# A hybrid decoder step on one core: when VectorE gets the next MLP weights' remainders, when the decode is held, and half of the split keys read back from memory

## The chip, the cores and the metric

The kernel runs on one core of a Trainium2 chip. The core has a matrix engine (TensorE; "PE" in the profile, its weight loads "PEld"), VectorE (DVE), ScalarE (ACT), GpSimd (POOL) and SyncE (SP), which here only issues transfers. Transfers are issued by SyncE, ScalarE and GpSimd into queues of their own, and 16 DMA engines carry them out. The metric is the device time of one execution in microseconds. The kernel before was run three times.

## The reference, cut to what matters

One layer of a decoder with width 1024 is computed for two groups of rows which share the weights: a prompt of 1024 tokens, and 8 samples of one token each with a cache of 8192 past tokens in pages of 128.

```python
h = rmsnorm(x) @ w_in                      # q, k, v (8 heads x 64), a forget logit per head, u, z
att = softmax(q k^T / 8 + c_q - c_k) v     # c: running sum of log_sigmoid(forget logit); causal
sgu = gelu(u) * (W_s z + b_s)              # gating in chunks of 128
x  += concat(rmsnorm(att), rmsnorm(sgu)) @ w_o
x  += cross_attention(rmsnorm(x)) @ w_co   # 4 heads into 256 memory tokens
h   = causal_conv3(rmsnorm(x) @ w_up)      # 2 x 2816 columns
x  += (silu(gate) * val) @ w_down
y   = rmsnorm(x)
```

All of it is float32. The keys, values, log forget gates, memory keys and values and the last convolution rows are returned too.

## The kernel before, in words

**Splitting.** A float32 product is made of three products of a faster format (`gemm3`, lines 265 to 272): each operand is split into a head `h`, a rounded copy made by ScalarE (line 233, or 236 with a scale), and a remainder `l = src - h`, made by VectorE (line 234 or 237). `wload` (line 250) loads a weight tile through SyncE into one of four `wr` buffers (line 247) and splits it into `wh` (five buffers) and `wl` (four).

**The prompt** goes through stages, in two halves of 512 tokens where this is possible: the input projections with the statistics of the norm (`p1`), attention of half 0 (`att0`, mixed with the memory's keys and values and the gating), attention of half 1 (`att1`), and then for each half `mid0`/`mid1` (merging of the heads, `out_proj` with `w_o`, cross-attention, `out_proj` with `w_co`) and `ffn0`/`ffn1` (the MLP, `ffn`). Half 1's merge is made beside the last `w_down` tiles of half 0's MLP (`side`).

**A stage's end.** `out_proj` makes the output in two column halves `n` of four row tiles `i`. Each tile's sum is added to the residual on VectorE (`residual`, line 953) and squared on ScalarE (line 228). Then `norm_T` (line 1016) transposes the result for the next product: TensorE's transposes (line 1028, and 1044 for the last row tile), each then split by ScalarE (line 236) and VectorE (line 237), first 8 times for the 384 columns of three row tiles, then 8 times for the last 128. The caller gives `first`, the next stage's first product, which is made on those columns as soon as they are there. In `ffn` this is tile 0 of `w_up`; the next tiles in its loop are 22, 1 and 23, as the gate's tiles (0 to 21) and the value's (22 to 43) alternate.

**Attention.** For each pair of heads `load` fetches queries, keys and values and `setup` prepares them: it transposes the queries (line 701) and the keys (line 726), splits them (ScalarE 707, 708, 730, GpSimd 732 or ScalarE 734; VectorE 721, 737), and fills in rows with the forget gates' sums by GpSimd's queue (709, 718). `setup` is a generator; the loop over the pair before advances it by a step after each score tile. Half 1 needs all 1024 keys, and there `setup` does the same to keys 0 to 511 (`kh == 0`) as half 0 did, and then to 512 to 1023. Raw keys, values, prepared operands and probabilities lie in 18 buffers `u` of 1024 columns; queries, small probabilities (the score tiles of half 0 among them) and outputs in 7 buffers `t2` of 520 columns. Half 1's first pair is prepared during half 0's last.

**The decode** of the 8 samples is a generator of its own (`sample`): 128 key steps and 128 value steps, each of which gathers 1 MB of the cache by an indirect transfer on GpSimd's queue (1333 and 1392) into one of four `kv` buffers. A key step multiplies on VectorE (line 1339) and reduces (line 1343); a value step is four matmuls (line 1398). Then come the samples' own projections (`sample_rest`).

**What sets the order.** The prompt is a generator too, and each of its yields tells how many microseconds of work it stands for. The loop at the end of `build` adds these up in `acc` and, whenever they reach the stage's `PACE`, takes a step from the decode, with at most `int(t / PACE) + 1` steps at one yield. While `held[0]` is set it takes none: from the last tile of an `out_proj`, and from the second half's first tile at the end of half 0's MLP, until `norm_T` ends or the stage is over. What was not taken stays in `acc`. The order in which instructions are traced is only their priority: a planner runs a cost model over the program, gives out buffers, and writes down one fixed order for each engine, in which an instruction that is ready sooner by that model may go ahead of one traced earlier. `tc.issue_after(x)` puts the instructions of a block behind `x` in their engine's order, without waiting for `x` to finish; the decode's key steps are put behind VectorE's newest instruction in this way (`behind`).

Of the kernel before, what the change touches and what calls it, by code (L numbers as in the profile page):

```python
# [79 lines left out]
def build(nc, tc, ctx, a, phases=None):  # L80
# [127 lines left out]
    cq_d = dram.tile([NH, 4, T], F32, tag="cq_d", name="cq_d")  # L208
    ck_d = dram.tile([NH, 4, T], F32, tag="ck_d", name="ck_d")
    an_d = dram.tile([T, AW], F32, tag="an_d", name="an_d")  # L210
    qs_d = dram.tile([NB, AW], F32, tag="qs_d", name="qs_d")
# [17 lines left out]

    def split(src, h, l, scale=None):  # L230

        if scale is None:
            nc.scalar.activation(h, src, AF.Copy)  # L233
            nc.vector.tensor_tensor(l, src, h.bitcast(F32), op=ALU.subtract)  # L234
        else:
            nc.scalar.activation(h, src, AF.Copy, scale=scale)
            nc.vector.scalar_tensor_tensor(l, src, scale, h.bitcast(F32), op0=ALU.mult, op1=ALU.subtract)  # L237
# [11 lines left out]

    def wload(src, n, raw=None):  # L250

        if raw is None:
            raw = wraw(src, n)
        l = spool.tile([P, SWID], F32R, tag="wl", bufs=WL, name=nm("wl"))[:, :n]
        h = spool.tile([P, SWID], F32R, tag="wh", bufs=WH, name=nm("wh"))[:, :n]
        if len(src.shape) == 3:
            h = h.rearrange("p (a b) -> p a b", b=src.shape[2])
            l = l.rearrange("p (a b) -> p a b", b=src.shape[2])
        split(raw, h, l)
        return h, l, raw  # L260
# [420 lines left out]
    def attention(hf, late=None, at=3):  # L681
# [3 lines left out]
        def load(hp):  # L685
            cs = slice(hp * P, (hp + 1) * P)
            qn = T2().rearrange("p (i c) -> p i c", c=P)
            nc.sync.dma_start(qn, q_d[hf * 512 : (hf + 1) * 512, cs].rearrange("(i p) c -> p i c", p=P))
            if hf == 0:
                kvn = U([P, 2 * nk, P])  # L690
                kn, vn = kvn[:, :nk, :], kvn[:, nk:, :]
            else:
                kn, vn = U([P, nk, P]), U([P, nk, P])
            nc.sync.dma_start(kn, k_d[: nk * P, cs].rearrange("(i p) c -> p i c", p=P))
            nc.sync.dma_start(vn, v_d[: nk * P, cs].rearrange("(i p) c -> p i c", p=P))
            return qn, kn, vn

        def setup(hp, qn, kn, vn):
# [4 lines left out]
            for j in range(2):  # L703
# [7 lines left out]
                if hf == 0:  # L711
                    kab = U([P, 2, 512], F32R)
                    ka.append(kab[:, 0, :])
                    kb.append(kab[:, 1, :])
                else:
                    ka.append(U([P, nk * P], F32R))
                    kb.append(U([P, nk * P], F32R))
                nc.gpsimd.dma_start(kb[j][64:68, :], ck_d[h, :, : nk * P])
            for j, qq in enumerate(qab):
                rows = slice(64 * j, 64 * j + 64)  # L720
                nc.vector.tensor_tensor(qq[64:128, 0, :], tr[rows, :], qq[0:64, 0, :].bitcast(F32), op=ALU.subtract)
            for kh in range(hf + 1):
                yield
                tr = (MS, BB, BA)[SB]()
                for i in range(4):
                    nc.tensor.transpose(tr[:, i * P : (i + 1) * P], kn[:, kh * 4 + i, :], ident)
                s = slice(kh * 512, kh * 512 + 512)
# [7 lines left out]
                for j in range(2):  # L735
                    rows = slice(64 * j, 64 * j + 64)
                    nc.vector.tensor_tensor(kb[j][0:64, s], tr[rows, :], ka[j][0:64, s].bitcast(F32), op=ALU.subtract)
            got.append((qab, ka, kb, vn))

# [221 lines left out]
    def out_proj(w, mh, ml, xt, fetch=None, ys=None):  # L961
# [19 lines left out]
        for n in range(2):  # L981
# [16 lines left out]
            for i in range(4):  # L998
# [14 lines left out]

                held[0] = n == 1 and i == 3
                yield 5.2 if n else 0.1
# [164 lines left out]
    def ffn(hf, xt, ys, late=None):  # L1180
# [5 lines left out]

        hs, ls = yield from norm_T(ys, G_FFN, lambda hs, ls, c: up(pv0[:, c], w0, hs, ls, c))
        if hf:
# [10 lines left out]
        for gi, gn in enumerate(GROUPS):  # L1199
            gh, gl = [], []  # L1200
            for f in range(f0, f0 + gn):
                hc2 = []
                for part in range(2):
# [3 lines left out]
                    if ft:  # L1207
                        w_, pv = wload(a["w_up"][ft], 1024), BK()
                        up(pv, w_, hs, ls, slice(0, 512))
                    else:  # L1210
                        pv = pv0
# [20 lines left out]
            for n in range(2):  # L1232
# [9 lines left out]
                for i in range(4):  # L1242
# [3 lines left out]
                    if f0 + gn < NF:  # L1246
                        xs_ = xt[i][:, n * 512 : (n + 1) * 512]
                        nc.vector.tensor_tensor(xs_, ps[:, :512], xs_, op=ALU.add)
                    else:
                        residual(xt, sq, i, n, ps)  # L1250
                    yield 3.9
                    if side and n:

                        held[0] = True
                        for _ in range(2):
# [546 lines left out]
    bgs.append(sample())  # L1802
    seen = 0
    for t in prompt():
# [6 lines left out]
        acc[0] += t  # L1811
        most = int(t / PACE[phase[1] or phase[0]]) + 1
        while bgs and not held[0] and most and acc[0] >= PACE[phase[1] or phase[0]]:
            most -= 1
            acc[0] -= PACE[phase[1] or phase[0]]
            w = next(bgs[0], None)
            if w is None:
                bgs.pop()
            else:
                acc[0] -= (w - 1) * PACE[phase[1] or phase[0]]  # L1820
        seen = len(nc.cur_bb.bb.instructions)
# [92 lines left out]
```

## Time and profile before

| | |
|---|---|
| time, median of 3 runs | 1885.33 us (1883.57 to 1890.65) |
| the profiled execution's own time | 1887.23 us |
| its span, first to last instruction | 1885.5 us |
| TensorE busy | 1810.9 us (96%) |
| VectorE busy | 1400.3 us (74%) |
| ScalarE busy | 755.7 us (40%) |
| GpSimd busy | 478.6 us (25%) |
| mean granted TensorE clock | 0.980 |
| moved by DMA | 517 MB, 274 GB/s |

All times within the execution are microseconds from the span's start. A timeline's line gives start, length, engine, line of the kernel, operation, output and inputs, and in brackets the engine's idle time before it with what ended it. A line of the waits gives who waited for whom, with total, times and longest. A line of the stretches gives the length, the busy time of each engine with its instructions, the granted clock of TensorE as a share of full speed, the DMA engines' share and the rate. Matmuls overlap, so that one of 512 columns is shown with 0.39 us or more although the next starts 0.23 us after it.

Where the stages lie in the trace: attention of half 0 up to about 390, of half 1 to 520, `w_o` of half 0 to 573, its cross-attention from there, `w_co` to 739, the MLP of half 0 to 1173, `w_o` of half 1 to 1228, `w_co` to 1393, the MLP of half 1 to the end.

### The profile page before, as it was taken

What the parts mean: (1) busy time and instruction counts of PE and PEld (TensorE: products, weight loads), DVE (VectorE), ACT (ScalarE), POOL (GpSimd) and SP (SyncE); (2) the same over time, 40 slices, a digit from 0 to 9 for tenths busy, and PEclk for the clock granted to TensorE, in tenths of its full rate; (3) what the DMA queues carried; (4) which work ended last, traced back from release to release, by engine and by line L of the source; (5) the groups of instructions that cost most, each with busy time, mean ns of one, the idle gap of its engine ahead of it and who ended that gap; (6) DMA issues with size and microseconds to landing.
All of it is one profiled execution on the core that took longest, in us unless ns stands there. A gap on an engine that the chain in (4) does not pass through costs nothing.

```text
span 1885.5 us, 24204 instructions
## 1 busy us (share of the span) xinstructions
PE 1810.9 (96%) x9255; PEld 1298.5 (69%) x9255; DVE 1400.3 (74%) x1672; ACT 755.7 (40%) x1371; POOL 478.6 (25%) x429
## 2 busy tenths in 40 slices
PE   8999999888898999999999999999999999999998
PEld 5987676556676667776777776765675668667765
DVE  4888678776687887889989898898865549654344
ACT  5332356565633444433324235234443333232232
POOL 1232332232121423313422322243322021101110
PEclk9999999988998999999999999999999999999999
DMA  8877888753396877659878888889869587678871
GB/s 319 286 259 269 326 314 290 287 182 105 132 384 229 328 272 280 257 201 375 301 280 314 284 320 328 344 319 349 308 242 346 196 294 260 253 218 286 321 253 59
DMA packets 156372, 517.07 MB, mean 274 GB/s; under 512 B 20168, under 2 KB 41928, under 8 KB 123488
## 3 DMA queue, kind: packets, MB, share of 16 engines
q0 software_dynamic: 56400, 339.04, 48.4%
q1 hardware_dynamic: 92944, 163.89, 25.1%
q10 hardware_dynamic: 6912, 12.59, 1.8%
q8 instruction: 73, 1.20, 0.2%
q14 instruction: 43, 0.35, 0.1%
HBM read 493.63 MB, written 21.84 MB: 273 GB/s over the span
## 4 chain that ended last, share of the span: by engine, by line
PE 84%; DVE 6%; DMA 4%; ACT 3%; issue 2%; POOL 1%; SPq 0%; DVEq 0%; POOLq 0%; ACTq 0%
PE ba L270 13%; PE ba L271 13%; PE ba L272 12%; PE bb L270 7%; PE bb L271 7%; PE bb L272 7%; PE dv L1398 6%; DVE kv L1339 1%; PE dv L1648 1%; DVE s L1343 1%; PE bb L796 1%; PE ba L994 1%; PE ba L996 1%; PE ba L995 1%; DMA wr<-w_ck 1%
## 5 line engine op out<-in xcount | busy, mean ns | idle before, releaser
L233 ACT ACTIVATE wh<-wr 128x1024 fp32r<-128x1024 f32 (+2 forms) x220 | 228.6, 1043 | 514.8 <-PE ba L271 173.5
L234 DVE TENSOR_TENSOR wl<-wr,wh 128x1024 fp32r<-128x1024 f32 (+2 forms) x220 | 263.1, 1201 | 127.5 <-PE ba L272 55.0
L1339 DVE TENSOR_TENSOR kv<-kv,d 128x1024 f32<-128x1024 f32 (+1 forms) x184 | 295.5, 1634 | 27.3 <-DMA kv<-cache_k,kidx 27.1
L1333 POOL DMA_INDIRECT kv<-cache_k,kidx x128 | 175.0, 1367 | 552.8 <-DVE s L1343 257.6
L1343 DVE TENSOR_REDUCE s<-kv 128x16 f32<-128x1024 f32 (+1 forms) x184 | 296.6, 1626 | 0.2
L1392 POOL DMA_INDIRECT kv<-cache_v,kidx x128 | 179.0, 1399 | 388.2 <-DVE s L1343 178.7
L270 PE MATMUL ba<-wh,u 128*128 128x512 f32 (+1 forms) x601 | 229.7, 384 | 3.1 <-DVE u L953 2.7
L271 PE MATMUL ba<-wl,u 128*128 128x512 f32 (+1 forms) x601 | 227.7, 379 | 0.0
L272 PE MATMUL ba<-wh,u 128*128 128x512 f32 (+1 forms) x601 | 224.9, 379 | 0.0
L270 PE MATMUL ba<-u,wh 128*128 128x512 f32 (+2 forms) x520 | 204.4, 394 | 0.4 <-DVE u L237 0.4
L271 PE MATMUL ba<-u,wh 128*128 128x512 f32 (+2 forms) x520 | 204.5, 394 | 0.0
L272 PE MATMUL ba<-u,wl 128*128 128x512 f32 (+2 forms) x520 | 203.2, 391 | 0.0
L1398 PE MATMUL dv<-kv,s 128*32 128x512 f32 x1024 | 136.5, 614 | 5.5 <-DMA kv<-cache_v,kidx 5.5
L270 PE MATMUL bb<-u,wh 128*128 128x512 f32 (+2 forms) x344 | 138.6, 403 | 0.7 <-DVE u L237 0.7
L270 PEld LDWEIGHTS ba<-wh,u 128*128 128x128 f32 x601 | 113.3, 189 | 37.6 <-issue 10.7
L271 PE MATMUL bb<-u,wh 128*128 128x512 f32 (+2 forms) x344 | 136.8, 399 | 1.5 <-DVE u L237 1.5
L272 PE MATMUL bb<-u,wl 128*128 128x512 f32 (+2 forms) x344 | 135.8, 395 | 0.0
L272 PEld LDWEIGHTS ba<-wh,u 128*128 128x128 f32 x601 | 113.1, 188 | 26.5 <-issue 5.0
L271 PEld LDWEIGHTS ba<-wl,u 128*128 128x128 f32 x601 | 113.3, 189 | 23.1 <-issue 2.5
L271 PEld LDWEIGHTS ba<-u,wh 128*128 128x128 f32 x520 | 99.3, 191 | 32.0 <-issue 12.2
L270 PEld LDWEIGHTS ba<-u,wh 128*128 128x128 f32 x520 | 99.3, 191 | 31.4 <-issue 8.4
L272 PEld LDWEIGHTS ba<-u,wl 128*128 128x128 f32 x520 | 99.1, 191 | 27.8 <-issue 8.0
(422 smaller groups left out, 3066.1 us busy)
## 6 DMA issues: line engine op xcount, KB each, us to landing
wr<-w_up SPq DMA_DIRECT2D x88, 512.0 KB
kv<-w_up POOLq DMA_DIRECT2D x22, 1024.0 KB, 6.7
wr<-w_down SPq DMA_DIRECT2D x40, 512.0 KB
kv<-w_down POOLq DMA_DIRECT2D x11, 1024.0 KB, 7.8
wr<-w_in SPq DMA_DIRECT2D x16, 512.0 KB
wr<-w_o SPq DMA_DIRECT2D x16, 512.0 KB
wr<-w_cq SPq DMA_DIRECT2D x16, 512.0 KB
wr<-w_co SPq DMA_DIRECT2D x16, 512.0 KB
```

What stands on the lines that cost most here:

```text
L233: nc.scalar.activation(h, src, AF.Copy)
L234: nc.vector.tensor_tensor(l, src, h.bitcast(F32), op=ALU.subtract)
L270: mmul(out, sh, mh, start=(i == 0), stop=False)
L271: mmul(out, sh, ml, start=False, stop=False)
L272: mmul(out, sl, mh, start=False, stop=(i == n - 1))
L796: mmul(po[64 * j : 64 * j + 64, q0:256], vn[:, kt, 64 * j : 64 * j + 64], pt[j][kt // 4][:, kt % 4, q0:256], start=(kt == 0), stop=(kt == ...
L994: mmul(pss[i], mh[k][:, tb], wh, start=(k == korder[0]), stop=False)
L1333: nc.gpsimd.indirect_dma_start(kv, None, a["cache_k"], off(kidx[:, b, ch : ch + 1]))
L1339: nc.vector.tensor_tensor(kvv[:, i : i + m, :], kvv[:, i : i + m, :], qb.unsqueeze(1).broadcast_to((P, m, 512)), op=ALU.mult)
L1343: nc.vector.tensor_reduce(s[:, ch * 4 + i : ch * 4 + i + m, :].rearrange("p k h -> p (k h)"), kvv[:, i : i + m, :].rearrange("p k (h d) -> ...
L1392: nc.gpsimd.indirect_dma_start(kv, None, a["cache_v"], off(kidx[:, b, ch : ch + 1]))
L1398: mmul(dv[32 * j : 32 * j + 32, :], s[:, ch * 4 : ch * 4 + 4, :].rearrange("p k h -> p (k h)"), kvv[:, j, :], start=(ch == 0), stop=(ch == ...
```

## The change

There are four parts.

1. `ffn` issues the loads of `w_up` tiles 22, 1 and 23 ahead of `norm_T`, and puts VectorE's subtraction for them behind marks: that of tile 22 behind VectorE's newest instruction after `first` on the first 384 columns, those of 1 and 23 behind its newest after `first` on the last 128. ScalarE's rounded copies are not bound.
2. The hold begins a tile sooner: in `out_proj` at `n == 1, i == 2`, and at the end of half 0's MLP with the last tile of `n == 0`.
3. The loop that takes decode steps has a `credit`: it grows with the prompt's yields, up to 1.2 paces (or one yield), and each step costs 0.75 of a pace; a step is taken only if it is there.
4. Half 0's attention stores the split keys of its 512 tokens (head and remainder) in a DRAM tile `ks_d`, by four transfers on GpSimd's queue for each pair. Half 1 reads them back on SyncE's queue, three transfers of 64 rows of 2 KB for each head (the head part twice), and transposes and splits only keys 512 to 1023. Its raw keys are half as many and lie in a `t2` buffer, not in a `u` buffer.

```diff
-    def split(src, h, l, scale=None):
+    def split(src, h, l, scale=None, after=None):
         if scale is None:
             nc.scalar.activation(h, src, AF.Copy)
-            nc.vector.tensor_tensor(l, src, h.bitcast(F32), op=ALU.subtract)
+            with tc.issue_after(after) if after else nullcontext():
+                nc.vector.tensor_tensor(l, src, h.bitcast(F32), op=ALU.subtract)
...
-                kn, vn = U([P, nk, P]), U([P, nk, P])
-            nc.sync.dma_start(kn, k_d[: nk * P, cs].rearrange("(i p) c -> p i c", p=P))
+                kn, vn = T2().rearrange("p (i c) -> p i c", c=P), U([P, nk, P])
+            nc.sync.dma_start(kn, k_d[hf * 512 : nk * P, cs].rearrange("(i p) c -> p i c", p=P))
...
                     ka.append(U([P, nk * P], F32R))
                     kb.append(U([P, nk * P], F32R))
+                    for r in range(2):
+                        nc.sync.dma_start(ka[j][64 * r : 64 * r + 64, 0:512].bitcast(F32), ks_d[h, :, 0, :])
+                    nc.sync.dma_start(kb[j][0:64, 0:512].bitcast(F32), ks_d[h, :, 1, :])
...
-            for kh in range(hf + 1):
+            for kh in (hf,):
...
+            if hf == 0:
+                for j in range(2):
+                    nc.gpsimd.dma_start(ks_d[hp * 2 + j, :, 0, :], ka[j][0:64, :].bitcast(F32))
+                    nc.gpsimd.dma_start(ks_d[hp * 2 + j, :, 1, :], kb[j][0:64, :].bitcast(F32))
...
-                held[0] = n == 1 and i == 3
+                held[0] = n == 1 and i >= 2
...
-        hs, ls = yield from norm_T(ys, G_FFN, lambda hs, ls, c: up(pv0[:, c], w0, hs, ls, c))
+        order = [f + part * NF for f in range(2) for part in range(2)][1:]
+        raws = {ft: wraw(a["w_up"][ft], 1024) for ft in order}
+        marks = []
+
+        def first(hs, ls, c):
+            up(pv0[:, c], w0, hs, ls, c)
+            marks.append(newest(ENG.DVE))
+
+        hs, ls = yield from norm_T(ys, G_FFN, first)
+        after = dict(zip(order, (marks[0], marks[1], marks[1])))
...
-                        w_, pv = wload(a["w_up"][ft], 1024), BK()
+                        w_, pv = wload(a["w_up"][ft], 1024, raws.pop(ft, None), after.pop(ft, None)), BK()
...
+                    held[0] = side is not None and (n == 1 or i == 3)
                     yield 3.9
                     if side and n:
-                        held[0] = True
...
-    seen = 0
+    seen, credit = 0, 0.0
...
-        most = int(t / PACE[phase[1] or phase[0]]) + 1
-        while bgs and not held[0] and most and acc[0] >= PACE[phase[1] or phase[0]]:
+        pace = PACE[phase[1] or phase[0]]
+        most, credit = int(t / pace) + 1, min(credit + t, max(1.2 * pace, t))
+        while bgs and not held[0] and most and acc[0] >= pace and credit >= 0.75 * pace:
             most -= 1
-            acc[0] -= PACE[phase[1] or phase[0]]
+            acc[0] -= pace
+            credit -= 0.75 * pace
```

More of the change, by code (lines that the diff above doesn't have):

```diff
@@ L209, in build @@
     ck_d = dram.tile([NH, 4, T], F32, tag="ck_d", name="ck_d")
+    ks_d = dram.tile([NH, 64, 2, 512], F32, tag="ks_d", name="ks_d")
     an_d = dram.tile([T, AW], F32, tag="an_d", name="an_d")
@@ L248, in wraw, with wload @@
         return raw
-    def wload(src, n, raw=None):
+    def wload(src, n, raw=None, after=None):
         if raw is None:
@@ L258, in wload @@
             l = l.rearrange("p (a b) -> p a b", b=src.shape[2])
-        split(raw, h, l)
+        split(raw, h, l, after=after)
         return h, l, raw
@@ L725, in setup @@
                 for i in range(4):
-                    nc.tensor.transpose(tr[:, i * P : (i + 1) * P], kn[:, kh * 4 + i, :], ident)
+                    nc.tensor.transpose(tr[:, i * P : (i + 1) * P], kn[:, i, :], ident)
                 s = slice(kh * 512, kh * 512 + 512)
@@ L1819, in build @@
             else:
-                acc[0] -= (w - 1) * PACE[phase[1] or phase[0]]
+                acc[0] -= (w - 1) * pace
         seen = len(nc.cur_bb.bb.instructions)
```

## The prediction

> **What bounds the kernel now.** I read the page first (busy shares, the clock row, the chain that ended last), then the busy time by stretch, then what TensorE waited for at each stage's end, and last the timelines of VectorE and TensorE there.
>
> ```profile
> span 1885.5 us, 24204 instructions
> PE 1810.9 (96%) x9255; PEld 1298.5 (69%) x9255; DVE 1400.3 (74%) x1672; ACT 755.7 (40%) x1371; POOL 478.6 (25%) x429
> ...
> PEclk9999999988998999999999999999999999999999
> ...
> PE 84%; DVE 6%; DMA 4%; ACT 3%; issue 2%; POOL 1%; SPq 0%; DVEq 0%; POOLq 0%; ACTq 0%
> ```
>
> TensorE is busy for 96% of the span and is 84% of the chain, so the change can win only where TensorE stands still or runs at a lower granted clock: 1885.5 - 1810.9 = 74.6 us of idle time. The next rows say where (columns: length, busy us of PE, PEld, DVE, ACT, POOL, clock, DMA share, GB/s).
>
> ```profile
> 400.00:520.00 120.00, 102.09 (x660) 72.21 (x661) 78.77 (x111) 70.38 (x143) 27.25 (x32) 0.89 0.43 147
> 573.00:603.00 30.00, 23.23 (x119) 19.53 (x117) 25.48 (x41) 9.93 (x22) 2.98 (x3) 0.83 0.58 198
> 739.00:759.00 20.00, 16.43 (x93) 14.36 (x91) 14.09 (x27) 11.71 (x27) 3.29 (x3) 0.91 0.59 211
> 1158.00:1180.00 22.00, 19.30 (x107) 13.79 (x107) 22.00 (x25) 14.14 (x26) 9.13 (x6) 1.00 0.91 330
> 1222.00:1250.00 28.00, 25.73 (x144) 18.61 (x142) 26.33 (x37) 12.03 (x23) 10.76 (x9) 0.94 0.85 305
> 1392.00:1412.00 20.00, 18.83 (x112) 15.79 (x111) 10.26 (x22) 11.63 (x24) 1.67 (x2) 1.00 0.50 202
> ...
> 759.00:1158.00 399.00, 398.95 (x1857) 289.26 (x1855) 365.12 (x339) 136.49 (x209) 113.80 (x82) 1.00 0.81 297
> ```
>
> The first row is the second half's attention; the next five are the five stage ends that the change touches: 30 - 23.2 = 6.8 us idle, then 3.6, 2.7, 2.3 and 1.2. Lower clock costs more: 30 x (1 - 0.83) = 5.1 us, 1.8, 0, 1.7, 0. The attention stretch has 17.9 idle and 120 x 0.11 = 13.2 of clock. In the last row, the first half's MLP, TensorE is never idle.
>
> **The change part by part.** *The remainders (MLP start).* Before, three `w_up` tiles beyond the first (22, 1, 23) have their remainder (line 234) taken on VectorE as soon as they land, in the middle of the stage end:
>
> ```profile
> 733.64 2.35 DVE L1339 TENSOR_TENSOR kv<-kv,d 128x1024 f32<-128x1024 f32 x2
> 739.17 1.22 DVE L234 TENSOR_TENSOR wl<-wr,wh 128x1024 fp32r<-128x1024 f32 x1
> 740.30 1.22 DVE L1343 TENSOR_REDUCE s<-kv 128x16 f32<-128x1024 f32 x1
> 741.43 1.22 DVE L234 TENSOR_TENSOR wl<-wr,wh 128x1024 fp32r<-128x1024 f32 x1
> 742.56 0.69 DVE L953 TENSOR_TENSOR u<-bb,u 128x512 f32<-128x512 f32 x1
> 743.16 1.22 DVE L234 TENSOR_TENSOR wl<-wr,wh 128x1024 fp32r<-128x1024 f32 x1
> ...
> 738.58 0.40 PE L271 MATMUL bb<-wl,u 128*128 128x512 f32 x1
> 738.81 0.40 PE L272 MATMUL bb<-wh,u 128*128 128x512 f32 x1
> 743.30 0.55 PE L1028 MATMUL bb<-cp,u 128*128 128x128 f32 x3 [2.45 <-DVE u L953]
> ...
> 738.15 6.58 SPq L247 DMA_DIRECT2D wr<-w_up  x4
> ```
>
> TensorE ended the last tile at 739.2, but its residual (line 953) started at 742.56: two remainders and half a decode reduction stood before it, and a third remainder behind it, ahead of the splits of the next transposes. TensorE waits 2.45 us for that residual's bank. After the change neither the three remainders nor this decode step (held, below) is there; line 953 can start near 739.2, 3.3 us sooner. The whole loss is 3.6 + 1.8 = 5.4; ScalarE, busy 11.7 of these 20 us, is late next, so I take 4.0 (0 to 5.4). At the other MLP start no key step is left and the idle is 1.2, so 0.8 (0 to 1.2). The early loads cost nothing: SyncE's four `w_up` loads were already issued at 738.15, before the transposes.
>
> The price: tiles 1 and 23 now have no remainder until the last of the 16 `norm_T` splits.
>
> ```profile
> 751.41 0.35 DVE L237 SCALAR_TENSOR_TENSOR u<-ba,gp,u 128x128 fp32r<-128x128 f32 x1 [0.99 <-ACT u L236]
> ...
> 758.70 0.35 DVE L237 SCALAR_TENSOR_TENSOR u<-ba,gp,u 128x128 fp32r<-128x128 f32 x1 [0.91 <-ACT u L236]
> ```
>
> Until then TensorE has tile 22 (24 matmuls, 0.23 us from start to start as at 738.58 and 738.81, 5.6 us) and the first tile's last 128 columns with their transposes (some 4 us), against the chain of these eight splits, 751.4 to 759.1. That cover nearly suffices; without it TensorE would wait for two remainders at 1.22 us, 2.4 per start. I take 0.5 at each, 1.0 in all (0 to 4.8).
>
> *The hold.* I counted decode steps through the loop's rule: when the hold begins at the five ends, 46, 62, 104, 112 and 129 steps have been issued before, 45, 61, 103, 110 and 128 after. So one key step leaves each of the first three ends (two line 1339 of 1.17 us and as much again in line 1343, some 4.5 us of VectorE) and two the fourth; at the fifth all 128 key steps are past. The first:
>
> ```profile
> 575.15 2.35 DVE L1339 TENSOR_TENSOR kv<-kv,d 128x1024 f32<-128x1024 f32 x2
> 577.42 1.13 DVE L237 SCALAR_TENSOR_TENSOR u<-ba,gp,u 128x384 fp32r<-128x384 f32 x2
> ...
> 578.08 1.54 PE L1028 MATMUL ba<-cp,u 128*128 128x128 f32 x6 [2.25 <-DVE u L237]
> 580.33 0.69 PE L270 MATMUL bb<-u,wh 128*128 128x384 f32 x1 [0.71 <-DVE u L237]
> 590.02 0.33 PE L1044 MATMUL bb<-cp,u 128*128 128x128 f32 x1 [2.19 <-DVE u L237]
> ```
>
> With that step gone the first two waits (2.25 + 0.71) should go, and their share of the clock loss, 5.1 x 2.96/6.8 = 2.2: 5.2 at most. The third stays, as the held step is the one that follows there next. I take 4.0 (0 to 5.2). At the end of the first MLP:
>
> ```profile
> 1162.20 2.33 DVE L1339 TENSOR_TENSOR kv<-kv,d 128x2048 f32<-128x2048 f32 x1
> 1170.29 2.25 DVE L1343 TENSOR_REDUCE s<-kv 128x32 f32<-128x2048 f32 x1
> 1173.20 0.50 PE L270 MATMUL ba<-wh,u 128*128 128x512 f32 x1 [2.53 <-DVE u L953]
> ```
>
> Two key steps overlap here; the hold, two tiles sooner, takes the second out: 2.5 (0 to 2.7). At the fourth end (1222 to 1250) VectorE is still working through steps issued well before the hold, as their loads came late (DMA share 0.85), so I take 1.0 of its 2.3 + 1.7 (0 to 4.0).
>
> *The even follow.* It spends the backlog at 1/0.75 of the pace at most. By my count the decode's main part ends 4 yields of the prompt later (index 403 for 399), the last step one sooner (460 for 461, of 470). What is moved goes to stretches where TensorE was never idle: 0. VectorE has 399 - 365 = 34 us free in the first MLP for one more step of 4.5 us.
>
> *The split keys.* The second half no longer transposes and splits the first 512 keys. In a head pair's preparation that work stands alone in the chain that ended last (start, length):
>
> ```profile
> 408.21 0.60 PE ba L726 x4
> 408.84 0.60 ACT u L730
> ...
> 410.79 0.69 DVE u L737
> ...
> 442.90 0.59 PE ba L726 x4
> ...
> 476.33 0.60 PE ba L726 x4
> ```
>
> Four transposes 0.6, two copies 1.2, two subtractions 1.4: 3.3 us from 408.21 to 411.48, in each of three pairs (the others begin at 442.90 and 476.33); the first pair, prepared during the first half, has the two copies to lose, 1.2: 11 at most. The least is the transposes alone, 4 x 0.6 = 2.4. GpSimd's eight copies go too. I take 6, about the middle, since the pair before can fill a part with its scores. New work: in the first half 16 stores on GpSimd's queue, at the price of the nearest issue there (below, 0.55 each, 9 us, GpSimd busy 25%), each behind VectorE's subtraction; only decode loads queue behind, and the decode gets 6 steps in that stage. In the second, 24 loads of 128 KB on SyncE, 3 MB less the 1 MB of keys no longer read, at a DMA share of 0.43: 0.
>
> ```profile
> L709 POOL DMA_DIRECT2D u<-cq_d x16: 518/555/642, 144.4 to 469.9; - x16
> ...
> 346.20 13.34 SPq L688 DMA_DIRECT2D t<-q_d  x2
> 392.25 0.38 SPq L688 DMA_DIRECT2D t<-q_d  x1
> ...
> 367.31 0.90 PE L780 MATMUL bb<-cp,t 128*128 128x128 f32 x3 [3.06 <-ACT t L759]
> ```
>
> The keys' raw tile moves to the `t2` pool of seven, which is short: a query load into it held SyncE's queue 13 us at 346, the next went out only at 392. Behind it wait the values and the next pair's loads. I take 1.0; the bound is the slower rival's.
>
> **The sum.** 4.0 + 0.8 + 4.0 + 2.5 + 1.0 + 6.0 = 18.3 gained, 1.0 + 1.0 lost: 16.3. The profiled execution took 1887.23, 1.9 above the median 1885.33; 1887.2 - 16.3 = 1870.9, and 1869 for the median.
>
> **A rule against part of this.** The row 573 to 603 has its clock at 0.83 though no single wait in it exceeds 2.25 us, and I counted clock as won back. The Trainium skill, TensorE: Matmul & The Clock Gate, Part 1: The HAM clock gate, says that the clock halves only after an idle window of about 3.4 us. By that rule closing short gaps gives back idle alone, the second rival below; the trace's row speaks rather against it.
>
> **The rivals.** (1) The preparation of keys is off the path: only 2.4 of the 6 comes, 1872.6. For it: VectorE, busy 78.8 of those 120 us, can put a decode step into the same place; against it: the chain rows above. (2) Gaps this short cost only themselves: without clock 2.5 and 3.0 at the two large ends, 4 in attention: 2.5 + 3.0 + 0.8 + 2.5 + 1.0 + 4.0 - 2.0 = 11.8, 1873.5. (3) ScalarE becomes the late one at the ends: about 1.0, 0.4, 1.0, 1.0, 0 there and 2.4 in attention, less 2.0: 3.8, 1881.5, no measurable change. For it: each transpose passes through its copy before VectorE's split; against it: it is busy 9.9 of 30 us at the first end. (4) Slower: the keys' raw tile holds a `t2` slot from about 360, the end of that 13 us wait, to its transposes, while the first half's last pair needs one for each of its eight score tiles. If each then opens a gap like the 3.06 us at 367, with clock in the stretch's proportion (13.2/17.9), that is 8 x 3.06 x 1.74 = 42 us, against the gain 1885.3 - 17.3 + 42 = 1910. Three gaps (16 us) eat the gain; it is slower by 0.5% from five on.
>
> **How the numbers follow.** 0.5% (9.4 us) is about what a measurement of this kernel can tell from no change. Forecast 0.40, rival 1 0.15, rival 2 0.10, rival 3 0.22, rival 4 0.13. Faster is the first three, 0.65; same 0.22; slower 0.13. All upper ends together are 29.5 gained, 1856; 4 more of the attention's clock, 1852, is the low end. The high end, 1892, holds rival 3 and the first gaps of rival 4. The forecast's own range is 1856 to 1876.
>
> **What would show it.** Right: at the MLP starts line 953 follows the last matmul within a microsecond, two line-234 subtractions come behind the last split; no line 1339 between the first projection's end and line 237; the attention stretch several microseconds shorter, with half of line 730's copies gone there. Wrong: TensorE waiting for line 234 behind the splits, for ScalarE at the ends, or for scores in 355 to 400 with SyncE held on `t2`.

## The result: slower, and the profile after

The changed kernel takes 1901.69 us (median of 5 runs, 1897.28 to 1903.98), the kernel before beside it 1886.02 (5 runs, 1883.57 to 1890.65): ratio 1.0069, 95% interval 1.0050 to 1.0089. That is 13 us slower by the ratio, where 16 us less were forecast, and beyond the range given. Below, a ratio times 1886 is written as microseconds.

The page of the changed kernel, whose profiled execution took 1903.98 us:

```profile
span 1902.2 us, 24264 instructions
...
PE 1816.6 (95%) x9239; PEld 1296.1 (68%) x9239; DVE 1393.8 (73%) x1664; ACT 751.7 (40%) x1365; POOL 477.5 (25%) x437
...
PE 77%; DMA 7%; DVE 7%; issue 5%; ACT 3%; POOL 1%; SPq 0%; DVEq 0%; POOLq 0%; ACTq 0%
```

TensorE's idle time is 1902.2 - 1816.6 = 85.6 us (74.6 before), and it is busy 5.7 us longer although it has 16 instructions less. So the loss has two parts, and only the larger one is idle time. The stretches of the changed kernel at the same places as those shown of before (the same columns):

```profile
400.00:520.00 120.00, 105.79 (x704) 76.08 (x705) 80.39 (x115) 74.12 (x149) 24.05 (x29) 0.93 0.61 194
561.00:591.00 30.00, 22.57 (x109) 18.03 (x108) 27.22 (x40) 11.58 (x23) 3.73 (x3) 0.83 0.60 202
739.00:759.00 20.00, 15.86 (x87) 13.85 (x85) 12.08 (x24) 10.89 (x26) 1.56 (x2) 0.91 0.23 80
1156.00:1178.00 22.00, 20.89 (x113) 15.55 (x112) 21.27 (x25) 14.19 (x26) 5.87 (x5) 1.00 1.02 388
1222.00:1250.00 28.00, 24.47 (x140) 18.20 (x139) 27.56 (x39) 10.70 (x22) 8.18 (x7) 1.00 0.81 298
1600.00:1620.00 20.00, 14.40 (x44) 9.59 (x43) 20.00 (x27) 4.20 (x7) 2.17 (x3) 0.79 0.60 189
```

Attention (first row) gained what the kept keys promised: 14.2 us idle for 17.9, the clock 0.93 for 0.89. The first two stage ends (second and third row) did not gain at all: 7.4 us idle for 6.8 and 4.1 for 3.6, at the same clocks. The end of the first MLP gained 1.6, the fourth end lost 1.3 of idle time and won back 1.7 of clock. And the last row is new: in the second MLP, where the kernel before has this,

```profile
1600.00:1620.00 20.00, 19.60 (x86) 15.55 (x85) 20.00 (x26) 7.94 (x11) 2.15 (x3) 1.00 0.51 170
```

TensorE now stands still for 5.6 us and its clock is at 0.79. The timeline of TensorE in the changed kernel shows for whom it waits:

```profile
1604.84 0.50 PE L272 MATMUL ba<-wh,u 128*128 128x512 f32 x1 [0.78 <-ACT u L234]
...
1606.73 0.49 PE L273 MATMUL ba<-wl,u 128*128 128x512 f32 x1 [1.39 <-DVE wl L236]
...
1607.39 0.50 PE L272 MATMUL ba<-wh,u 128*128 128x512 f32 x1 [0.17 <-DVE t L1235]
...
1615.10 1.22 PE L274 MATMUL ba<-wh,u 128*128 128x512 f32 x2 [2.00 <-DVE u L236]
...
1618.01 0.79 PE L272 MATMUL ba<-wh,u 128*128 128x512 f32 x1 [1.27 <-DVE t L1235]
```

And that of VectorE shows what stood in its way there, lines 1587 and 1589, the product and the sums of the sample's cross-attention with its memory keys:

```profile
1607.33 2.33 DVE L1589 TENSOR_REDUCE sS<-kv 128x4 f32<-128x1024 f32 x2
...
1610.31 2.35 DVE L1587 TENSOR_TENSOR kv<-kv,d 128x1024 f32<-128x1024 f32 x2
...
1613.24 1.21 DVE L236 TENSOR_TENSOR wl<-wr,wh 128x1024 fp32r<-128x1024 f32 x1
...
1614.97 2.33 DVE L1589 TENSOR_REDUCE sS<-kv 128x4 f32<-128x1024 f32 x2
```

VectorE is full (20.00 of 20). The remainder for which TensorE waits at 1615.10 is made at 1614.37, directly behind the one at 1613.24, and has had two such pairs in front of it. The generator of the sample gives each of these eight steps the weight 3 (it yields 3). The loop charges the backlog `acc` three paces for it, but the new `credit` only 0.75 of one.

### The profile page after: what moved, and what is told of

Read it like the earlier page. It is cut to its first block, busy times and chain, and to the rows that moved or that the text cites. A ratio compares the mean times of both kernels' runs of the same rounds, so it can differ in the third digit from the quotient of the medians.

```text
span 1902.2 us, 24264 instructions
## 1 busy us (share of the span) xinstructions
PE 1816.6 (95%) x9239; PEld 1296.1 (68%) x9239; DVE 1393.8 (73%) x1664; ACT 751.7 (40%) x1365; POOL 477.5 (25%) x437
## 4 chain that ended last, share of the span: by engine, by line
PE 77%; DMA 7%; DVE 7%; issue 5%; ACT 3%; POOL 1%; SPq 0%; DVEq 0%; POOLq 0%; ACTq 0%
PE ba L272 12%; PE ba L273 11%; PE ba L274 11%; PE bb L272 6%; PE bb L273 6%; PE bb L274 6%; PE dv L1417 6%; DVE kv L1358 2%; DMA kv<-cache_k,kidx 1%; DMA qs_d<-t 1%; PE dv L1667 1%; PE ba L1110 1%; DVE s L1362 1%; PE bb L789 1%; PE ba L1003 1%
```

## The experiments

All ratios are to the kernel before on the same chip, with 95% intervals; the medians of the kernel before were 1884.9 to 1888.9 us over the five groups of runs.

**The credit, and its charge.** Theory A: the credit lets the weight-3 steps run back to back. The first run takes the credit out of the changed kernel.

```diff
-        while bgs and not held[0] and most and acc[0] >= pace and credit >= 0.75 * pace:
+        while bgs and not held[0] and most and acc[0] >= pace:
```

> The changed kernel with the pacing loop of before (no credit); hold, late remainders and kept keys stay. Theory A (the credit charges a step by 0.75 of a pace whatever its weight, so the sample's eight cross-memory steps of weight 3 run back to back at 1604 to 1630 and overload VectorE): by the loop's rule these steps fall at yields 408, 411, 413, 414, 416, 418, 419, 421 instead of 415 to 419, so the 10.3 us lost there come back and TensorE is busy over 19 of 20 us in that stretch: about 1891. Rival B (the longer hold alone makes the overload, because it leaves a backlog of 24 in place of 16): the loss stays, about 1901. If the 5.61 us wait for o_mk in the first cross-attention goes too, the credit made that as well, and the time comes to about 1883.

Measured: 1882.61 us, ratio 0.9973 (0.9961 to 0.9985). Not 10 but 18 us came back, and the result is below the kernel before; this is the expectation's last case, and the wait of 5.61 us for memory keys in the first cross-attention is gone too (2.17 and 0.93 us there, both for copies by ScalarE). The second run keeps the credit and charges it by weight.

```diff
                 acc[0] -= (w - 1) * pace
+                credit -= (w - 1) * 0.75 * pace
```

> The changed kernel, with the credit charged by the step's weight as the backlog already is: only the order of the sample's steps from yield 415 on changes (weight-3 steps at 415, 417, 418, 419, 421, 422, 423, 425 instead of 415 to 419, the last step of the sample at 466 instead of 460 of 470). Theory A: the 10.3 us at 1604 to 1630 come back, less what the six yields' later end costs at the tail (0 to 6): 1891 to 1897. Rival B (the hold's backlog, or the loads' lateness, makes the overload): about 1901. Everything ahead of 1600, the wait for o_mk among it, stays as it was.

Measured: 1893.01 us, 1.0031 (1.0020 to 1.0042), 7 us less than the changed kernel. Its stretch at the same place:

```profile
1600.00:1620.00 20.00, 19.68 (x86) 15.68 (x85) 19.55 (x23) 4.54 (x8) 2.71 (x4) 1.00 0.68 239
```

The idle time is gone and the clock is full, with VectorE almost as busy (19.55 of 20). Theory A holds for this place: it is the bunching, not the amount. It leaves 11 of the credit's 18 us open. One part of the expectation did not hold: ahead of 1600, where the steps leave at the same yields, the first cross-attention waits 3.82 us for a copy by ScalarE, not 5.61 for the load.

**The keys.** Part 4 of the change alone on the kernel before, and the changed kernel without part 4.

```diff
-            for kh in range(hf + 1):
+            for kh in (hf,):
```

> The kernel before with the kept split keys alone. Theory C (the keys gain some 10 us by the end of the second half's attention, and the first cross-attention's later wait for o_mk is another part's doing): 1874 to 1879. Rival D (the kept keys shift the loads so that o_mk is late in cross-attention whatever the rest): the wait of about 5 us at its first transposes and the lower clock around it are there too, 1884 to 1888.

> The changed kernel without the kept split keys. Theory C: it loses the 10 us of attention and keeps the wait for o_mk and the overload in the second MLP: about 1911. Rival D: the loss of attention's 10 us and the gain of about 10 at o_mk cancel: about 1902. The overload at the weight-3 steps (10 us) is there by both.

Measured: keys alone 1879.8 us, 0.9950 (0.9934 to 0.9967); the changed kernel without them 1913.08, 1.0120 (1.0101 to 1.0140). Both say 9.4 to 9.6 us gained, whatever the rest does. Theory C holds for the size; but keys alone also waits 2.2 us at the memory keys of cross-attention where before waits 1.1, so that wait is not another part's doing alone.

**The other parts alone.** The hold (part 2), the remainders (part 1), the keys with the remainders, the credit (part 3), each on the kernel before:

```diff
-                held[0] = n == 1 and i == 3
+                held[0] = n == 1 and i >= 2
```

> The kernel before with the sooner hold alone. The prediction's step (4.0 + 2.5 + 1.0 us gained): about 1880 where before has 1887.7. Theory F (the gaps at the stage ends are refilled by the next late thing: TensorE's waits for VectorE's splits behind the first projection, a decode load at the first MLP's end; and the backlog that the hold leaves must be worked off in the next stage): 1886 to 1892.

> The kernel before with the later remainders alone. The prediction's step (4.0 + 0.8 gained, 1.0 lost): about 1884. Theory G (the residual of line 953 follows at once, but TensorE then waits as long for the first split, because ScalarE's copy of the fourth weight tile waits for its load ahead of the split's copy): within 1 us of before, 1887 to 1889.

> The kernel before with the kept keys and the later remainders, without hold and credit. Keys alone took 1879.8, keys with remainders and hold 1882.6. If the hold is what costs (theory F), 1876 to 1880; if the remainders are (theory G with a loss), 1882 to 1885.

> The kernel before with the credit alone (its hold, keys and remainders of before). The prediction's step: 0, about 1888. Theory A (bunched weight-3 steps; by the rule they fall two each at yields 415 and 416, one each at 417, 419, 421, 422): half to all of the 10 us at that place, 1893 to 1900. If it costs as much as the 19 us that taking it out of the changed kernel gave, 1905: then it loses in other stages too, not through the hold's backlog.

Measured: hold 1892.97 us, 1.0047 (1.0027 to 1.0066); remainders 1884.29, 0.9992 (0.9974 to 1.0009); keys and remainders 1876.17, 0.9950 (0.9932 to 0.9968); credit 1894.31, 1.0047 (1.0030 to 1.0065). So keys -9.4 us, remainders -1.5, hold +8.9, credit +8.9: in sum +6.9 of the 13, and 6 come from parts together. Put in one after the other they are: keys and remainders -9.4 (the remainders add nothing to the keys), the hold on top +4.3 (0.9950 to 0.9973), the credit on top of that +18.1 (to 1.0069). One reason may be that the sooner hold leaves the credit a larger backlog (33.8 against 25.0 at yield 413, two yields before the weight-3 steps, by the loop's rule); no run shows this by itself.

The remainders alone do at the first MLP's start what was forecast. This stretch of that kernel has 1.9 us idle for 3.6 and the clock at 1.00 for 0.91, 3.5 us in all:

```profile
739.00:759.00 20.00, 18.13 (x106) 14.95 (x106) 15.96 (x29) 14.43 (x30) 3.24 (x4) 1.00 0.56 197
```

The whole kernel shows at most 1.5 of it, within its interval. For the hold, VectorE's timeline of the kernel with the hold alone tells what happened at the first end:

```profile
575.01 1.13 DVE L238 SCALAR_TENSOR_TENSOR u<-ba,gp,u 128x384 fp32r<-128x384 f32 x2
...
577.99 0.16 DVE L1079 TENSOR_SCALAR rq<-rn0r 128x4 f32<-128x4 f32 x1
578.06 2.35 DVE L1340 TENSOR_TENSOR kv<-kv,d 128x1024 f32<-128x1024 f32 x2
580.33 0.61 DVE L238 SCALAR_TENSOR_TENSOR u<-bb,gp,u 128x384 fp32r<-128x384 f32 x1
...
583.04 2.35 DVE L1340 TENSOR_TENSOR kv<-kv,d 128x1024 f32<-128x1024 f32 x2
```

and TensorE's:

```profile
585.71 0.47 PE L1045 MATMUL ba<-cp,u 128*128 128x128 f32 x1 [2.59 <-DVE u L238]
587.09 0.48 PE L1045 MATMUL bb<-cp,u 128*128 128x128 f32 x1 [0.91 <-DVE u L238]
```

The first splits at 575.01 follow the residual at once, as forecast. But the step held back runs at 578.06, with another behind it at 583.04, between the splits that are left. It stands directly behind line 1079, a small scaling that is traced after `norm_T` and that the planner has moved ahead of the last 11 of the 16 splits. A step taken after the hold is put behind VectorE's newest instruction, here this one, so the hold's end does not keep it out of the stage end. (In the kernel before, the first step after the hold follows the same scaling, line 1078, in the same way, at 584.84.) The wait has moved from 578.08 (2.25 us in the kernel before) to 585.71. The waits over 0.3 us at that end are 7.2 us in sum, 6.6 before: nothing gained. This doesn't explain 8.9 lost. This kernel's span is 7.4 us longer (1892.9). Idle time is 5.0 of it (79.6 for 74.6), but its clock, 0.982 for 0.980, takes some 3.6 off again (1 - clock, times the span). So about 6 us more lie in TensorE's busy time, at the same work. Of the idle time, 3.7 us lie between 1590 and 1680, where the weight-3 steps stand (4.06 idle for 0.40). In the stretch shown above TensorE waits 2.09 and 1.97 us for VectorE, which is full here too:

```profile
1600.00:1620.00 20.00, 15.94 (x69) 12.34 (x68) 20.00 (x28) 6.36 (x11) 2.12 (x3) 1.00 0.61 210
```

By the loop's rule these steps only move by two yields at most; why this costs 3.7 us was not found.

**What lies in TensorE's busy time.** The rows of line 1687 (1706 in the changed kernel), the sample's eleven `w_down` steps, give the answer. Busy time of this line alone, from 1740 to the end, in the kernel before (columns: length, PE, PEld, clock, DMA share, GB/s):

```profile
1740.00:1900.00 160.00, 13.53 (x88) 3.11 (x88) 0.98 0.55 196
```

and in the changed kernel; the hold alone, the credit alone and the changed kernel without credit have the same 18.99:

```profile
1740.00:1900.00 160.00, 18.99 (x88) 4.19 (x88) 1.00 0.58 211
```

The same 88 matmuls take 5.5 us more. TensorE's timeline of the kernel before shows why:

```profile
1803.80 1.06 PE L1687 MATMUL dv<-kv,d 128*32 128x512 f32 x4
1804.68 1.04 PE L1687 MATMUL ms<-kv,d 128*32 128x512 f32 x4
...
1808.17 1.08 PE L1687 MATMUL dv<-kv,d 128*32 128x512 f32 x8
1809.06 1.06 PE L1687 MATMUL ms<-kv,d 128*32 128x512 f32 x8
```

Each product is 32 columns wide, stands in one of TensorE's four groups of 32 columns and shows as two matmuls. A step has two products for each half of the result (`dv` and `ms`), in two of the groups; the two take 1.06 us (x4). Where two steps go out together, their four fill all four groups and take 1.08 us (x8). Before, the eleven steps stood in 7 places (four pairs and three single steps); with the hold or the credit nearly all stand alone, in 10. Theory P: this place is the cost. First the steps were asked for in pairs, with the weight 2.

```diff
-            yield 1
+            if f2 % 4 == 2 or f2 == NF - 2:
+                yield 2 if f2 % 4 == 2 else 1
```

> The changed kernel; the sample's eleven w_down steps go out two at a time (each pair weighs 2, so the pace is kept). Theory P (the matmuls of one such step fill two of the four column groups and take as long as those of two steps together: 10 places of 1.8 us in the changed kernel, 7 in the kernel before, because the hold and the credit spread the steps one to a yield): 6 places, about 7 us less, ratio about 1.003. Rival (these matmuls stand beside work that TensorE has to do anyway, their place is no cost): no change, 1.007.

> The kernel before with kept keys and later remainders (0.995 of before) and the w_down steps in pairs: the kernel before has 7 places, so theory P gives only 1 x 1.9 us, ratio about 0.994; the rival 0.995.

> The changed kernel with the credit charged by weight (1.0031 alone) and the w_down steps in pairs: theory P takes 11 places to 6, 8.9 us, ratio about 0.998, which is what the changed kernel without credit has (0.9973). If it stays above 1.001, the credit costs something that is in neither the weight-3 steps nor the pairs.

> The kernel before with the sooner hold alone (1.0047) and the w_down steps in pairs: theory P gives 7 us less, ratio about 1.001; what stays above 0.999 (the kernel before would also gain 1.9 us) is the 3.7 us more of idle time at 1590 to 1680. Rival (the hold's loss is all waits): 1.0047.

Measured: 1894.55 us, 1.0051 (1.0034 to 1.0068); 1879.78, 0.9972 (0.9955 to 0.9989); 1889.07, 1.0014 (0.9997 to 1.0031); 1891.72, 1.0025 (1.0009 to 1.0040). Three gained 3 to 4 us where 7 to 9 were expected, and the second lost 4 where 2 were to be gained. The edit failed in its aim: 9 places or more remained. By the loop's rule the eleven steps leave in 6 or 7 yields in the kernel before, the changed kernel, and those with the hold or the credit alone, so it is not the loop that parts them, and pairing there had little to join. What the traces show is GpSimd's order: before, the later loads of `w_down` are issued two together (at 1810.42, 1818.04 and 1827.08), in the changed kernel one at a time (1828.03, 1833.31, 1837.91, 1841.56), each behind matmuls of an earlier `w_down` step. What turned pairs into single steps was not found. The second of these kernels, which had 7 places without the edit, shows the cost from the other side:

```profile
1740.00:1900.00 160.00, 17.31 (x88) 3.74 (x88) 0.98 0.45 162
```

Its `w_down` takes 3.8 us more than in the kernel without the pairs (13.53 there too), and the whole 0.0022 or 4.1 us more. So the places cost time here too, but the theory wanted an edit that doesn't depend on the planner's order. Each step's four products were then spread over all four groups, two for each half of the result, in turn:

```diff
                 f = f2 + q
-                j = f % 4
                 for n in range(2):
+                    j = (q * 2 + n) ^ (f2 // 2 % 2)
```

> The changed kernel; each of the sample's w_down steps spreads its four products over all four column groups of TensorE (two rows of weights times two halves of the result), where they used two groups, twice each. Theory P (a place of these matmuls costs about 1.85 us however many groups it fills, and by half that where four products run together): the group, now 18.4 us in 10 places, takes about 10, 8 us less, ratio about 1.0027. Rival (their place is no cost, the loss is waits): no change, 1.007.

> The kernel before with kept keys, later remainders and the w_down products on four column groups: 13.1 us in 7 places go to about 10, 3 us less than the 0.995 of the kernel without them: about 0.9935. Rival: 0.995.

> The changed kernel without the credit (0.9973; its w_down matmuls take 18.4 us) and these on four column groups: 8 us less, about 0.993. If the hold were no loss besides their place, it comes level with the kernel that has keys and remainders and four groups (about 0.9935). If the hold also costs waits (3.9 us of idle time at 1590 to 1680), it stays 2 to 4 us above it.

> The kernel before with the w_down products on four column groups alone: by theory P 3 us less, 0.9984; the rival 1.0.

Measured: 1890.95 us, 1.0018 (1.0002 to 1.0035); 1876.99, 0.9937 (0.9914 to 0.9960); 1874.81, 0.9927 (0.9903 to 0.9950); 1884.46, 0.9983 (0.9966 to 0.9999). Expected were 1.0027, 0.9935, 0.993 and 0.9984. The changed kernel with four groups has, for this line,

```profile
1740.00:1900.00 160.00, 11.30 (x88) 1.93 (x88) 0.98 0.55 201
```

and in its timeline a step's four products start within 0.02 us, and their second matmuls 0.46 us later:

```profile
1814.61 0.62 PE L1706 MATMUL dv<-kv,d 128*32 128x512 f32 x1
1814.62 0.62 PE L1706 MATMUL ms<-kv,d 128*32 128x512 f32 x1
1814.62 0.62 PE L1706 MATMUL dv<-kv,d 128*32 128x512 f32 x1
1814.63 0.62 PE L1706 MATMUL ms<-kv,d 128*32 128x512 f32 x1
1815.07 0.59 PE L1706 MATMUL dv<-kv,d 128*32 128x512 f32 x1
```

The Trainium skill, TensorE: Matmul & The Clock Gate, Part 3: Packing small matmuls, says that products which write to different groups of 32 columns run at the same time in the array; the rows above agree. Theory P stands: 7.7 us of the line's time (18.99 to 11.30) brought 9.6 us of the whole; in the other three kernels, in the order above, 2.6 us of the line brought 2.5, 7.7 brought 8.7, and 2.6 brought 3.2. The third kernel tells what is left of the hold: with this cost out of the way, keys, remainders and hold (0.9927) are not above keys and remainders (0.9937), and the intervals overlap. It still stands idle for 3.9 us between 1590 and 1680, where the second kernel does for 0.8, but for 72.8 us in the whole, against 75.4. So beside keys and remainders the hold comes out about even; alone, it was not run with four groups.

**The rest of the credit.** With four groups the credit still costs 17 us (1.0018 against 0.9927). Two runs part it, both with four groups: the credit charged by weight, and the credit only while the decode runs.

```diff
-        while ... and credit >= 0.75 * pace:
+        while ... and (phase[1] or credit >= 0.75 * pace):
```

> The changed kernel with the w_down products on four column groups and the credit charged by weight. From 1.0031 (weight alone) the 11 places' 20.2 us go to about 10.5: 0.998. The two corrections are then additive and what is left above 0.9927 (the same kernel without credit), 10 us, is the credit's part in the decode: its loads meet those of the two cross-attentions later, with waits of 3.8 us for o_mk and 5 us for cache_v.

> The changed kernel with the w_down products on four column groups and the credit only while the decode runs, not in the sample's remaining layers. By the loop's rule the weight-3 steps fall at yields 411 (two), 413, 414, 416, 418, 419, 421. If the credit's whole loss were in the sample's steps: 0.9927. If the decode's part costs 10 us as the kernel with the credit by weight leaves it: 0.998. In between, the part above 0.9927 is the decode's.

Measured: 1885.01 us, 0.9972 (0.9957 to 0.9987), and 1886.84, 0.9983 (0.9966 to 1.0000). Both sit where the decode's share was expected, 8 to 11 us above 0.9927: of the credit's 17 us, 7 to 9 are in the sample's steps after the decode and 8 to 11 in the decode ahead of them. Where, the stretches around the two cross-attentions show, first of the kernel without credit,

```profile
625.00:765.00 140.00, 134.41 (x657) 96.33 (x656) 108.12 (x138) 69.94 (x149) 34.73 (x31) 0.99 0.69 258
1270.00:1420.00 150.00, 147.15 (x728) 97.72 (x728) 127.66 (x163) 74.11 (x149) 53.78 (x41) 1.00 0.82 317
```

then of the one with the credit in the decode only:

```profile
625.00:765.00 140.00, 132.33 (x637) 95.35 (x636) 105.97 (x140) 67.97 (x145) 37.51 (x30) 0.98 0.72 264
1270.00:1420.00 150.00, 143.36 (x698) 95.88 (x697) 124.35 (x157) 72.21 (x146) 50.68 (x39) 0.98 0.80 301
```

Idle time is 2.1 and 3.8 us more, and the clock costs 1.4 and 3.0: 10.3 of the 11.0 us between the two spans (1881.7 and 1870.7). By the loop's rule the credit brings decode steps out later in the first cross-attention, the seventh to ninth after the hold at yields 204, 205 and 208 rather than 202, 203 and 207. GpSimd's timeline of the kernel without credit has no load of the decode in the 20 us in which cross-attention's last memory keys and `w_co` are loaded (SyncE issues these from 640 on):

```profile
637.25 0.94 POOL L1352 DMA_INDIRECT kv<-cache_k,kidx  x1 [2.72 <-DVE s L1362]
...
657.11 0.94 POOL L1411 DMA_INDIRECT kv<-cache_v,kidx  x1 [18.93 <-DVE s L1362]
```

With the credit three stand in them:

```profile
643.83 4.95 POOL L1352 DMA_INDIRECT kv<-cache_k,kidx  x1 [2.70 <-PE dv L1417]
...
649.08 0.94 POOL L1411 DMA_INDIRECT kv<-cache_v,kidx  x1 [0.30 <-issue]
...
651.08 0.94 POOL L1352 DMA_INDIRECT kv<-cache_k,kidx  x1 [1.06 <-DVE s L1362]
```

What waits then differs from kernel to kernel: in the changed kernel TensorE waited 5.61 us at 661.92 for the memory keys, in this one 3.81 us at 657.93 for a copy by ScalarE, which is behind a maximum that VectorE gave late. In this kernel a decode step stands in front of that maximum (line 1112) on VectorE:

```profile
645.64 2.32 DVE L1358 TENSOR_TENSOR kv<-kv,d 128x1024 f32<-128x1024 f32 x2
...
649.02 0.67 DVE L1112 TENSOR_REDUCE cmx<-ba 128x2 f32<-128x512 f32 x1
```

In the kernel without credit VectorE stands idle for 1.80 us before the same maximum, at 647.61, and the decode step comes only at 651.64. So here VectorE's work is in the chain, in the changed kernel a load is; how much of the 8 to 11 us each of them costs was not told apart.

## Why the prediction was wrong, point by point

- **The even follow, "What is moved goes to stretches where TensorE was never idle: 0".** This step failed: the term was put at 0, and the credit costs 8.9 us alone and 17 to 18 in the changed kernel. Four things were missed. The steps were counted, not weighed: "at most 1/0.75 of the pace" holds only for steps of weight 1, and eight of them weigh 3 and cost the credit no more. A stretch where TensorE is never idle may still have VectorE full (20.00 of 20 at 1600 in the kernel before), and then a bunch of moved steps becomes TensorE's idle time (5.6 us there). In the decode, steps moved into the two cross-attentions, where TensorE does wait, cost 8 to 11 us; whether by their loads or by VectorE's work stays open. And the sentence that the change "can win only where TensorE stands still or runs at a lower granted clock" left out that TensorE's busy time at equal work can change: `w_down` steps that stand alone cost 5.5 us more, with the credit or with the hold.
- **The hold, 4.0 + 2.5 + 1.0.** Alone it costs 8.9. The first waits went as forecast, but "the third stays" was too kind: the held steps come out between the later splits, behind an instruction that the planner runs early, and the waits come to 7.2 for 6.6. The end of the first MLP did lose its wait of 2.53 for the residual, though the kernel without credit then waited 4.03 there for a decode load. The loss is in stages that the prediction did not count for the hold: the `w_down` places (5.5 us) and the idle time between 1590 and 1680 (3.7 us). Beside keys and remainders it costs 4.3, and with the `w_down` products on four groups it is about even.
- **The remainders, 4.0 + 0.8 - 1.0.** At the first start 3.5 us came when this was done alone, 4.0 forecast; at most 1.5 show in the time, and none beside the keys (0.9950 with and without them). In the changed kernel they came to nothing there, as the third rival had it. The residual follows the last matmul at once, in VectorE's timeline:

```profile
737.73 0.69 DVE L962 TENSOR_TENSOR u<-bb,u 128x512 f32<-128x512 f32 x1 [3.15 <-PE bb L274]
742.11 0.62 DVE L239 SCALAR_TENSOR_TENSOR u<-ba,gp,u 128x384 fp32r<-128x384 f32 x1 [3.69 <-ACT u L238]
...
756.77 2.35 DVE L236 TENSOR_TENSOR wl<-wr,wh 128x1024 fp32r<-128x1024 f32 x2
```

  but then VectorE waits 3.69 us for ScalarE's first copy, which stands in its queue behind a weight tile's copy that waits for its load:

```profile
739.94 1.06 ACT L234 ACTIVATE wh<-wr 128x1024 fp32r<-128x1024 f32 x1 [1.97 <-DMA wr<-w_up]
...
741.52 0.56 ACT L238 ACTIVATE u<-ba,gp 128x384 fp32r<-128x384 f32 x1
```

  The two late remainders sit behind the last split at 756.77, as forecast.
- **The keys, 6.0 gained, 1.0 lost for the `t2` pool.** The mechanism was right and the size too small: 9.4 net alone, 9.6 in the changed kernel, within the 2.4 to 11 given. The slower rival, queries and keys starving the `t2` pool in 355 to 400, did not come. This stretch of the changed kernel has 8.7 us of idle time, where the kernel before has 10.8 (34.16 busy):

```profile
355.00:400.00 45.00, 36.34 (x229) 24.32 (x229) 35.39 (x72) 30.75 (x80) 14.42 (x18) 0.89 0.67 193
```

  The time came out on that rival's side by other mechanisms.
- **The clock.** It was counted as won and lost with short gaps, and that held in part: in the changed kernel's stretch 1600 to 1620 the clock is 0.79 with no single wait over 2.00 us, and full once the waits were gone. But with the hold alone the same stretch has 4.1 us idle, in two waits of 2.09 and 1.97 us, at a clock of 1.00, so short gaps do not always cost clock, and the second rival is right in such places. The Trainium skill, TensorE: Matmul & The Clock Gate, Part 1: The HAM clock gate, has the clock fall after an idle window of about 3.4 us. Here five waits of 0.17 to 2.00 us, 5.6 in sum within 14 us, were enough, so the "only" in the prediction is not borne out; what separates the two cases was not found.
- **The sum.** Right in kind for the keys and too small (5.0 forecast, 9.4 measured), too high for the remainders (at most 1.5 of 3.8), wrong in sign for the hold, and 0 for a credit that cost more than all the rest won: -9.4 for keys and remainders, +4.3 for the hold, +18.1 for the credit give the 13.

The fastest version found keeps the split keys, the late remainders and the hold, drops the credit, and spreads `w_down` over four column groups: 1874.81 us, 0.9927 of the kernel before (0.9903 to 0.9950; the one without the hold, 0.9937, lies within this).

## What to carry to other kernels

A step of background work that is moved must be counted with its weight on every engine that it uses, and above all on the one that runs full where it lands. TensorE never being idle in a stretch does not mean that there is room: another engine may be full there, and TensorE's own time for a moved step may grow. A hold does not pay if its backlog still comes out before the stage end is past, and a mark behind the newest instruction is only as late as the planner runs that instruction; a hold that keeps the steps out for longer was not tried. An edit to the pacing should be judged by the busy time of the moved lines as well as by waits.

## What the hardware showed that was not expected

- A product of 32 columns costs its time whether or not its neighbours fill the other groups: two products 1.06 us, four 1.08. So the same 88 matmuls took 13.5 to 20.9 us of TensorE's busy time, by nothing but which steps stood together, and 10.9 to 12.3 once each step filled all four groups; no wait shows it.
- Waits of 2.00 us and less, 5.6 us within 14, lowered the granted clock to 0.79 over 20 us; two waits of 2.09 and 1.97 us, 4.1 within 6.2 us, left it at 1.00.
